# Next chunk's down weights issued behind the fifth product's operands, a gap in phase one's buffers, and the early out projection's split rows kept as two tiles

## The chip, the cores and the metric

The kernel runs on one core of a Trainium2 chip. The metric is the time of one execution on the device, in microseconds (us). Five engines work side by side, each in its own program order: TensorE (PE, matmuls; PEld is its weight loading), VectorE (DVE), ScalarE (ACT), GpSimd (POOL) and SyncE (SP), which here only issues DMA transfers. They wait for each other through semaphores.

## The reference, cut to what matters

A decoder of two layers on 1024 tokens of width 1024, in float32. Each layer is

```python
h = rms_norm(x, attn_norm[l])
proj = h @ w_in[l]
q_a, k_a, v_a, u_b, cq_c, ckv_c, kr_c = jnp.split(proj, split_idx, axis=-1)
out_a = swa_mixer(q_a, k_a, v_a, ...)     # sliding window of 128, 6 heads
out_b = pool_mixer(u_b, ...)              # trailing means over 2, 4, 8, 16
out_c = mla_mixer(cq_c, ckv_c, kr_c, ...) # causal latent attention, 6 heads
mixed = jnp.concatenate([out_a, out_b, out_c], axis=-1)   # width 1024
x = x + mixed @ w_out[l]
h = rms_norm(x, ffn_norm[l])
x = x + (jax.nn.silu(h @ w_gate[l]) * (h @ w_up[l])) @ w_down[l]   # hidden width 2816
```

## The kernel before, in words

Every float32 operand of a matmul is split into two parts, hi (a rounding cast on ScalarE) and lo (operand minus hi, a subtract on VectorE); the helper `split` (L58) does both. A product is then three matmuls: hi·hi, hi·lo and lo·hi.

A layer runs through four stages. Phase one makes the norm, the input projection with weights `wb` and `wa` and the first two mixers. Phase two makes the latent attention; the out projection is done in two parts there: `early_out` (rows 0 to 4 of the eight k-tiles, the first two mixers' output, L890) and `late_out` (the rest). `early_out` is issued at a low priority (offset -3000), so that its matmuls come in between those of the attention. For each of 2 column halves and 8 token tiles it splits five k-tiles of `xm` into one tile `mh` of 128 x 2 x 5 x 128, takes 15 matmuls (L886 to L888, in `outmm`) into `po`, adds `po` to the residual `stage` on VectorE (L907) and stores it. Its `mh` has one buffer in the pool `low`.

Then `gate_up` and `down` make the feed-forward part by a scheme of seven products of half-size blocks in place of eight. `gate_up` writes the token operands of the down products, already split, to a scratch `gd` in device memory (`gd<-go`, L1278).

`down` runs over 11 pairs of row blocks of `w_down` in four chunks of 2, 3, 3 and 3 pairs. A chunk does seven products in the order 1, 2, 5, 6, 3, 7, 4, each of 4 token tiles x its pairs x 3 matmuls, 24 in the first chunk and 36 in the others. What the text calls the fifth product is the fifth in this order (product 3), the sixth is product 7. A product needs

- its token operand `ga`, one 512 KB load per pair (L1041, from `gd`, issued by SyncE),
- its weight operand `op`, a cast on ScalarE (L1043) and a subtract on VectorE (L1044) of a block of `rw`, for some products after subtracts of blocks on GpSimd (L1034).

`rw` are the chunk's weight rows, 512 KB each (L1026): 4 for the first chunk, 6 for each of the others, in two buffers. The first chunk also reads back the residual rows (`xm<-xp`, L1050), and drains `kept`, the last pair's splits and stores of `gate_up` (the `go` subtracts on VectorE, `gd<-go` on SyncE).

The order on each engine is made by a scheduler from the order in which the program is written, its priorities and a simulated time. Of the loads, all are issued by SyncE in that order. A DMA may be tied behind another instruction by `tc.issue_after(...)`. Buffers lie in pools that are placed one behind the other; `gap` (L51) opens a pool that holds nothing but a filler of a given number of bytes per partition, written once by a one-element memset on GpSimd. Phase one has two, of 1024 and 2176 bytes.

Of the kernel before, what the change touches and what calls it, by code (L numbers as in the profile page):

```python
# [12 lines left out]
F32R = mybir.dt.float32r  # L13
# [8 lines left out]
P = 128  # L22
# [303 lines left out]
def phase1(nc, tc, A, l, pool, split, f, bcast, G):  # L326
    ve, sc, gp, te, sy = nc.vector, nc.scalar, nc.gpsimd, nc.tensor, nc.sync
    cosT, sinT = G["cosT"], G["sinT"]
    ident, xm, xrow, krr = G["ident"], G["xm"], G["xrow"], G["krr"]
    with ExitStack() as ph:  # L330
        gap = G["gap"]
# [14 lines left out]
        hp = [pool(ph, f"p1h_{l}"), hq]  # L346
        early = pool(ph, f"p1e_{l}")
        wj = pool(ph, f"p1j_{l}")
        wt = pool(ph, f"p1t_{l}")
        wz = pool(ph, f"p1z_{l}")  # L350
        ps_mm = pool(ph, f"p1mm_{l}", bufs=2, space=PSUM)
# [21 lines left out]
        hTs, rows = {}, {}  # L373
        behind = []
        ahead = {}
# [20 lines left out]
        with tc.high_priority() if l == 0 else nullcontext():  # L396
# [4 lines left out]
            for i, (c0, n) in enumerate(((0, 512), (512, 400), (912, 400))):  # L401
                for k in range(KT):
                    raw = early.tile([P, 512], F32, name="raw", bufs=5 if l else 11)[:, 0:n]
                    dma(raw, A["w_in"][l, k * P : (k + 1) * P, c0 : c0 + n])
                    hi, lo = wcol(0, k, c0, n), wcol(1, k, c0, n)
# [30 lines left out]
        for t in range(NT):  # L436
# [3 lines left out]
            hT, r = hTs[t], rows[t]  # L440
# [41 lines left out]
            for a in range(2):  # L482
                top, low = slice(64 * a, 64 * a + 64), slice(64 - 64 * a, 128 - 64 * a)
# [60 lines left out]
            if t % 2 == 1:  # L544
                W = 16 + 2 * P
                for k in range(2):
# [26 lines left out]
                    po = ps_o.tile([P, 512], F32, name="po")  # L573
# [16 lines left out]
            for g in range(2):  # L590
# [3 lines left out]
                for i0, ni in ((0, 2), (2, 1)):  # L594
                    s = ps_sc.tile([P, 2, 256], F32, name="s")
                    for i in range(i0, i0 + ni):
                        h = 3 * g + i
# [6 lines left out]
                for i in range(3):  # L604
                    h = 3 * g + i
# [3 lines left out]
                for i in range(3):  # L609
                    h = 3 * g + i  # L610
# [19 lines left out]
def phase2(nc, tc, A, l, pool, split, f, bcast, G):  # L630
# [3 lines left out]
    with ExitStack() as ph:  # L634
# [248 lines left out]
        def outmm(po, mh, ml, wo, nk):  # L883
            for k in range(nk):
                wh, wl = wo[k]
                te.matmul(po, mh[:, k], wh, start=k == 0, stop=False)  # L886
                te.matmul(po, mh[:, k], wl, start=False, stop=False)  # L887
                te.matmul(po, ml[:, k], wh, start=False, stop=k == nk - 1)  # L888

        def early_out():  # L890
            for n in range(2):
                c = slice(512 * n, 512 * n + 512)
                wo = []
                for k in range(5):
                    raw = stage(512)
                    rows(raw, k, c)
                    w = (fill if k else low).tile([P, 2, 512], F32R, name=f"wo{k}")
                    split(w[:, 0], w[:, 1], raw)
                    wo.append((w[:, 0], w[:, 1]))
                for t in range(NT):  # L900
                    xt = stage(512)
                    sy.dma_start(xt, G["xsrc"][t * P : (t + 1) * P, c])
                    mh = low.tile([P, 2, 5, P], F32R, name="mh")
                    split(mh[:, 0], mh[:, 1], xm[:, t, 0:5])
                    po = ps_p.tile([P, 512], F32, name="po3")
                    outmm(po, mh[:, 0], mh[:, 1], wo, 5)
                    ve.tensor_tensor(out=xt, in0=xt, in1=po, op=ALU.add)  # L907
                    sy.dma_start(xp[t][:, c], xt)

# [91 lines left out]
def down(nc, tc, A, l, pool, split, f, G, banks, gd, xres, out):  # L1001

    ve, sc, gp, te, sy = nc.vector, nc.scalar, nc.gpsimd, nc.tensor, nc.sync
    xrow, xp = G["xrow"], G["xp"][l]
    last = l == DEPTH - 1
    LEFT, RIGHT = slice(0, 512), slice(512, 1024)
    with ExitStack() as ph:  # L1010
        sg = pool(ph, f"p5s_{l}", bufs=4)
        ac = pool(ph, f"p5a_{l}")
        a1 = ac.tile([P, 4, 512], F32, name="a1")
        a5 = ac.tile([P, 4, 512], F32, name="a5")
        a6 = ac.tile([P, 4, 512], F32, name="a6")
        even = pool(ph, f"p5e_{l}", bufs=2)
        G["go"] = pool(ph, f"p5g_{l}", bufs=2)
        sw = pool(ph, f"p5w_{l}", bufs=3, side="right")

        def load(ps, rp):  # L1020
            h = len(ps)
            rw = rp.tile([P, 2 * h, D], F32, name="rw")
            for b in range(2):
                for j, i in enumerate(ps):
                    r = (2 * i + b) * P
                    sy.dma_start(rw[:, b * h + j], A["w_down"][l, r : r + P, :])  # L1026
            q = {f"B{a + 1}{b + 1}": rw[:, a * h : a * h + h, c] for a in range(2) for b, c in enumerate((LEFT, RIGHT))}
            return ps, q, h

        def chunk(loaded, first, final, ahead=None):  # L1030
            ps, q, h = loaded

            def sub(o, a, b):
                gp.tensor_tensor(out=o, in0=a, in1=b, op=ALU.subtract)  # L1034

            ops, nxt = {}, []

            def operands(at, p, b):
                ga = sg.tile([P, 3, 2, 512], F32R, name="ga")
                for j, i in enumerate(ps):  # L1040
                    sy.dma_start(f(ga[:, j]), gd[i][at])  # L1041
                t = sw.tile([P, 2, 3, 512], F32R, name="op")[:, :, 0:h]
                sc.copy(t[:, 0], q[b])  # L1043
                ve.tensor_tensor(out=t[:, 1], in0=q[b], in1=f(t[:, 0]), op=ALU.subtract)  # L1044
                ops[p] = ga, t

            def rows(ts, n):
                if first:
                    for t in ts:
                        sy.dma_start(xrow[t], xp[t])  # L1050
                    for _ in range(n):
                        next(G["kept"], None)

            operands(0, 1, "B11")
            operands(1, 2, "B21")
            rows(range(4), 0)
            sub(q["B12"], q["B12"], q["B11"])
            operands(2, 5, "B12")
            rows(range(4, 6), 7)
            if ahead is not None:  # L1060
                nxt.append(ahead())
            sub(q["B12"], q["B22"], q["B12"])
            operands(3, 6, "B12")
            rows(range(6, 8), 0)
            if first:
                for t in range(4, NT):
                    gp.tensor_tensor(out=xrow[t][:, LEFT], in0=xrow[t][:, LEFT], in1=xrow[t][:, RIGHT], op=ALU.subtract)
            sub(q["B11"], q["B12"], q["B11"])
            sub(q["B21"], q["B21"], q["B12"])
            operands(4, 3, "B22")  # L1070
            operands(5, 7, "B11")
            operands(6, 4, "B21")

            def add(o, a, eng=ve):
                eng.tensor_tensor(out=o, in0=o, in1=a, op=ALU.add)

            for at, p in enumerate((1, 2, 5, 6, 3, 7, 4)):
                S_, T_ = ops[p]
                for i in range(4):
                    lo, hi = xrow[i], xrow[i + 4]  # L1080
                    n = 4 * at + i
                    acc = banks[n % 8 > 4].tile([P, 512], F32, name="dn", tag=("gu", "dn")[n % 8 > 4])
                    ts = slice(i * P, (i + 1) * P)
                    for j in range(h):
                        te.matmul(acc, S_[:, j, 0, ts], T_[:, 0, j], start=j == 0, stop=False)  # L1085
                        te.matmul(acc, S_[:, j, 0, ts], T_[:, 1, j], start=False, stop=False)  # L1086
                        te.matmul(acc, S_[:, j, 1, ts], T_[:, 0, j], start=False, stop=j == h - 1)  # L1087
                    dst = (a1[:, i], lo[:, LEFT], lo[:, RIGHT], hi[:, LEFT], a5[:, i], a6[:, i], hi[:, RIGHT])[p - 1]
                    if first and p in (1, 5, 6):
                        sc.copy(dst, acc)  # L1090
                    else:
                        add(dst, acc)
                    if not final:
                        continue
                    if p == 1:
                        add(lo[:, LEFT], a1[:, i], gp)
                    elif p == 6:
                        add(a6[:, i], a1[:, i], gp)
                        add(hi[:, LEFT], a6[:, i], gp)
                        add(a5[:, i], a6[:, i], ve)  # L1100
                        add(lo[:, RIGHT], a5[:, i], ve)
                    elif p == 7:
                        add(hi[:, LEFT], hi[:, RIGHT], ve)
                        add(hi[:, RIGHT], a5[:, i], ve)
                    if p in (3, 4):
                        t = i if p == 3 else i + 4
                        dst = out[0] if last else xres
                        sy.dma_start(dst[t * P : (t + 1) * P, :], xrow[t])
            return nxt

        with ExitStack() as st:
            first = load(range(0, 2), pool(st, f"p5z_{l}", side="right"))
            nxt = chunk(first, True, False, lambda: load(range(2, 5), even))
        nxt = chunk(nxt[0], False, False, lambda: load(range(5, 8), even))
        nxt = chunk(nxt[0], False, False, lambda: load(range(8, 11), even))
        chunk(nxt[0], False, True)


# [271 lines left out]
```

## Time and profile before

| what | value |
|---|---|
| median of 3 runs | 2178.31 us (2177.22 to 2181.81) |
| profiled execution, its own time | 2177.97 us |
| its span in the trace | 2176.1 us |
| mean granted clock of TensorE | 0.99 |
| matmul stretch of `down`, layer 0 | 874.4 to 1090.5 us |
| matmul stretch of `down`, layer 1 | 1956.0 to 2171.2 us |
| stretch of `early_out`'s blocks, layer 0 and 1 | about 170 to 345, 1259 to 1425 us |

The page names an instruction by its line, engine, and what it writes and reads (`dn<-op,ga`: the down product's sum from weight operand and token operand). Times in a timeline are microseconds from the span's start. The number in brackets behind a row is the time for which the engine stood idle before it, with the instruction or transfer that ended the wait. DMA rows on SyncE show the issue; "us to landing" is from issue until the data is there.

### The profile page before, as it was taken

Reading aid. Unit: us, or ns where it says so; the run is one execution under the profiler, and the core shown is the slowest. Engines: PE = TensorE matmul, PEld = TensorE weight load, DVE = VectorE, ACT = ScalarE, POOL = GpSimd, SP = SyncE. Lnnn points to the kernel's source line nnn. Section 1 sums busy time; section 2 is a strip of 40 time slices with the busy share of each in tenths; the row PEclk is TensorE's granted clock in tenths of the full one; section 3 lists DMA queues with packets and bytes.
Section 4 is the critical chain, followed back from the end, with each engine's and each line's share of the span. In section 5 each row is a group of like instructions: output and inputs, shape, how many; then the busy total and the mean of one; then the engine's idle time right before and its main releaser. Section 6 shows DMA issues by size and latency. Waiting matters only on the chain.

```text
span 2176.1 us, 29696 instructions
## 1 busy us (share of the span) xinstructions
PE 2096.3 (96%) x10423; PEld 1756.8 (81%) x10423; DVE 1689.1 (78%) x2595; ACT 1084.4 (50%) x2301; POOL 976.0 (45%) x916
## 2 busy tenths in 40 slices
PE   8998999999999999999989989999999999999999
PEld 6886898877888888788878868888778888887887
DVE  6567888799888887765756678887998878877657
ACT  7777676663434333321267777766534443333111
POOL 2445456256544452522624354552654545436215
PEclk9999999999999999999999999999999999999999
DMA  7002211324445335975530122113144344369754
GB/s 232 1 1 97 92 45 49 117 87 145 164 144 176 136 136 194 411 300 196 204 105 1 37 93 83 49 59 128 69 158 169 138 156 151 140 229 406 272 200 164
DMA packets 133732, 312.16 MB, mean 143 GB/s; under 512 B 13071, under 2 KB 63952, under 8 KB 133584
## 3 DMA queue, kind: packets, MB, share of 16 engines
q1 hardware_dynamic: 133396, 310.19, 39.8%
q8 instruction: 83, 1.36, 0.2%
q14 instruction: 65, 0.53, 0.1%
q10 hardware_dynamic: 188, 0.08, 0.0%
HBM read 203.53 MB, written 106.70 MB: 143 GB/s over the span
## 4 chain that ended last, share of the span: by engine, by line
PE 45%; DVE 7%; DMA 5%; issue 2%; ACT 2%; POOL 1%; SPq 0%; DVEq 0%; ACTq 0%; POOLq 0%
PE dn L1085 5%; PE dn L1086 5%; PE dn L1087 5%; PE gu L1240 5%; PE gu L1239 5%; PE gu L1238 5%; PE acc L446 2%; PE acc L447 2%; PE acc L448 2%; DMA ga<-gd 1%; DMA rw<-in_w_down_dram 1%; PE tp L847 1%; PE po L888 1%; PE po L886 1%; PE po L887 1%
## 5 line engine op out<-in xcount | busy, mean ns | idle before, releaser
L1240 PE MATMUL gu<-T,sb 128*128 128x512 f32 x704 | 274.8, 391 | 9.0 <-DVE sb L58 8.8
L1238 PE MATMUL gu<-T,sb 128*128 128x512 f32 x704 | 274.9, 390 | 4.9 <-DVE B L58 2.0
L1239 PE MATMUL gu<-T,sb 128*128 128x512 f32 x704 | 274.0, 389 | 0.0
L1085 PE MATMUL dn<-op,ga 128*128 128x512 f32 x616 | 240.6, 392 | 8.5 <-DMA ga<-gd 8.5
L1086 PE MATMUL dn<-op,ga 128*128 128x512 f32 x616 | 240.7, 391 | 0.0
L1087 PE MATMUL dn<-op,ga 128*128 128x512 f32 x616 | 239.9, 391 | 0.0
L58 ACT CAST go<-xm 128x512 fp32r<-128x512 f32 x154 | 94.8, 620 | 264.5 <-POOL xm L1272 98.6
L1034 POOL TENSOR_TENSOR rw<-rw 128x1536 f32<-128x1536 f32 (+1 forms) x32 | 110.9, 3477 | 245.3 <-DVE op L1044 156.3
L1043 ACT CAST op<-rw 128x1536 fp32r<-128x1536 f32 (+1 forms) x56 | 76.9, 1376 | 284.9 <-PE dn L1087 266.6
L1215 POOL TENSOR_TENSOR xm<-raw 128x512 f32<-128x512 f32 x44 | 68.1, 1550 | 322.3 <-DMA raw<-in_w_up_dram 110.5
L58 DVE TENSOR_TENSOR go<-xm,go 128x512 fp32r<-128x512 f32 x154 | 155.8, 1021 | 34.2 <-ACT go L58 30.1
L58 ACT CAST sb<-raw 128x512 fp32r<-128x512 f32 x180 | 110.1, 617 | 118.0 <-PE gu L1240 97.2
L1240 PEld LDWEIGHTS gu<-T,sb 128*128 128x128 f32 x704 | 132.1, 188 | 40.4 <-DVE sb L58 13.1
L1238 PEld LDWEIGHTS gu<-T,sb 128*128 128x128 f32 x704 | 132.1, 188 | 35.2 <-ACT sb L58 3.5
L58 DVE TENSOR_TENSOR sb<-raw,sb 128x512 fp32r<-128x512 f32 x180 | 157.2, 874 | 1.3 <-ACT sb L58 0.3
L1272 POOL TENSOR_TENSOR xm<-xm 128x512 f32<-128x512 f32 x88 | 142.6, 1628 | 30.1 <-DVE go L58 19.3
L1239 PEld LDWEIGHTS gu<-T,sb 128*128 128x128 f32 x704 | 132.2, 188 | 27.2
L1044 DVE TENSOR_TENSOR op<-rw,op 128x1536 fp32r<-128x1536 f32 (+1 forms) x56 | 114.4, 2044 | 39.1 <-ACT op L1043 36.1
L1085 PEld LDWEIGHTS dn<-op,ga 128*128 128x128 f32 x616 | 116.4, 189 | 34.5 <-issue 7.3
L1087 PEld LDWEIGHTS dn<-op,ga 128*128 128x128 f32 x616 | 116.2, 189 | 24.6
L1086 PEld LDWEIGHTS dn<-op,ga 128*128 128x128 f32 x616 | 116.5, 189 | 24.0
L1238 PE MATMUL gu<-B,A 128*128 128x512 f32 x336 | 131.5, 391 | 2.8 <-ACT B L58 2.8
(332 smaller groups left out, 6071.4 us busy)
## 6 DMA issues: line engine op xcount, KB each, us to landing
gd<-go SPq DMA_DIRECT2D x154, 512.0 KB, 3.1
ga<-gd SPq DMA_DIRECT2D x154, 512.0 KB, 5.9
raw<-in_w_gate_dram SPq DMA_DIRECT2D x22, 1024.0 KB, 5.6
raw<-in_w_up_dram SPq DMA_DIRECT2D x22, 1024.0 KB, 6.2
rw<-in_w_down_dram SPq DMA_DIRECT2D x44, 512.0 KB, 8.7
xp<-stage SPq DMA_DIRECT2D x32, 256.0 KB, 2.0
old<-xp SPq DMA_DIRECT2D x16, 512.0 KB, 4.2
xp<-xm SPq DMA_DIRECT2D x16, 512.0 KB, 2.9
```

What stands on the lines that cost most here:

```text
L58: return sc.copy(hi, src), ve.tensor_tensor(out=lo, in0=src, in1=f(hi), op=ALU.subtract)
L1034: gp.tensor_tensor(out=o, in0=a, in1=b, op=ALU.subtract)
L1043: sc.copy(t[:, 0], q[b])
L1044: ve.tensor_tensor(out=t[:, 1], in0=q[b], in1=f(t[:, 0]), op=ALU.subtract)
L1085: te.matmul(acc, S_[:, j, 0, ts], T_[:, 0, j], start=j == 0, stop=False)
L1086: te.matmul(acc, S_[:, j, 0, ts], T_[:, 1, j], start=False, stop=False)
L1087: te.matmul(acc, S_[:, j, 1, ts], T_[:, 0, j], start=False, stop=j == h - 1)
L1215: gp.tensor_tensor(out=s1, in0=q["A21"], in1=q["A22"], op=ALU.add)
L1238: te.matmul(acc, s[:, 0, k], b[:, 0, k], start=k == 0, stop=False)
L1239: te.matmul(acc, s[:, 0, k], b[:, 1, k], start=False, stop=False)
L1240: te.matmul(acc, s[:, 1, k], b[:, 0, k], start=False, stop=k == HK - 1)
L1272: gp.tensor_tensor(out=q[o], in0=q[a], in1=q[b], op=op)
```

## The change

It has three parts. In `down`, the loading of the next chunk's weights moves from behind the third product's operands to behind the fifth's, and each of its transfers is tied behind the one before it, the first behind the last `ga` load of the fifth product; the second group of residual rows moves behind the fourth product's operands. In phase one a third filler of 384 bytes is opened ahead of the pools of `wa` and of most of `wb`. In `early_out`, the split rows are kept as two tiles, `mh0` with three k-tiles and `mh3` with two, each with its own cast and subtract, of the same size together as `mh`.

```diff
@@ phase one
         wj = pool(ph, f"p1j_{l}")
+        gap(ph, f"p1m_{l}", 384)
         wt = pool(ph, f"p1t_{l}")
@@ early_out
-                    mh = low.tile([P, 2, 5, P], F32R, name="mh")
-                    split(mh[:, 0], mh[:, 1], xm[:, t, 0:5])
+                    parts = []
+                    for a, b in ((0, 3), (3, 5)):
+                        mh = low.tile([P, 2, b - a, P], F32R, name=f"mh{a}")
+                        split(mh[:, 0], mh[:, 1], xm[:, t, a:b])
+                        parts += [(mh[:, 0, k], mh[:, 1, k]) for k in range(b - a)]
                     po = ps_p.tile([P, 512], F32, name="po3")
-                    outmm(po, mh[:, 0], mh[:, 1], wo, 5)
+                    for k in range(5):
+                        (hi, lo), (wh, wl) = parts[k], wo[k]
+                        te.matmul(po, hi, wh, start=k == 0, stop=False)
+                        te.matmul(po, hi, wl, start=False, stop=False)
+                        te.matmul(po, lo, wh, start=False, stop=k == 4)
@@ down, load
-        def load(ps, rp):
+        def load(ps, rp, pin=None):
...
-                    sy.dma_start(rw[:, b * h + j], A["w_down"][l, r : r + P, :])
+                    with tc.issue_after(pin.ins) if pin else nullcontext():
+                        pin = sy.dma_start(rw[:, b * h + j], A["w_down"][l, r : r + P, :])
@@ down, chunk
+            pin = []
...
-                    sy.dma_start(f(ga[:, j]), gd[i][at])
+                    pin[:] = [sy.dma_start(f(ga[:, j]), gd[i][at])]
...
             operands(2, 5, "B12")
-            rows(range(4, 6), 7)
-            if ahead is not None:
-                nxt.append(ahead())
             sub(q["B12"], q["B22"], q["B12"])
             operands(3, 6, "B12")
+            rows(range(4, 6), 7)
             rows(range(6, 8), 0)
...
             operands(4, 3, "B22")
+            if ahead is not None:
+                nxt.append(ahead(pin[0]))
             operands(5, 7, "B11")
             operands(6, 4, "B21")
```

SyncE in the first chunk of `down` of layer 0, from the second `ga` load of the fourth product on (the names `gd_0_4` and `gd_1_4` are the fifth product's operands of pairs 0 and 1, `gd_10_0` a store by `gate_up`), in the program of before:

```order
L1041 DMA ga<-gd_1_3_5617 128x1024
L1050 DMA xm<-xp_83 128x1024
L1026 DMA rw<-in_w_down_dram 128x1024 x3
L1050 DMA xm<-xp_84 128x1024
L1278 DMA gd_10_0_5677<-go 128x1024
L1050 DMA xm<-xp_85 128x1024
L1026 DMA rw<-in_w_down_dram 128x1024 x2
L1278 DMA gd_10_1_5678<-go 128x1024
L1026 DMA rw<-in_w_down_dram 128x1024 x2
L1041 DMA ga<-gd_0_4_5611 128x1024
L1041 DMA ga<-gd_1_4_5618 128x1024
L1026 DMA rw<-in_w_down_dram 128x1024 x5
```

The same place in the program of the change:

```order
L1051 DMA ga<-gd_1_3_5671 128x1024
L1060 DMA xm<-xp_83 128x1024
L1060 DMA xm<-xp_84 128x1024
L1288 DMA gd_10_0_5731<-go 128x1024
L1060 DMA xm<-xp_85 128x1024
L1288 DMA gd_10_1_5732<-go 128x1024
L1051 DMA ga<-gd_0_4_5665 128x1024
L1051 DMA ga<-gd_1_4_5672 128x1024
L1035 DMA rw<-in_w_down_dram 128x1024 x6
L1051 DMA ga<-gd_0_5_5666 128x1024
L1051 DMA ga<-gd_1_5_5673 128x1024
L1288 DMA gd_10_2_5733<-go 128x1024
```

The seven weight rows ahead of the fifth product's operands are gone from there, and six stand between those and the sixth product's.

VectorE at the same time, from the third product's weight split on (`op`, L1044; `go` is `gate_up`'s last token operand, `xm<-xm,dn` the adding of a product's result), before:

```order
L1044 TENSOR_TENSOR op<-rw,op 128x1024
L1075 TENSOR_TENSOR xm<-xm,dn 128x512 x4
L1044 TENSOR_TENSOR op<-rw,op 128x1024
L58 TENSOR_TENSOR go<-xm,go 128x512
L1044 TENSOR_TENSOR op<-rw,op 128x1024
L58 TENSOR_TENSOR go<-xm,go 128x512
L1044 TENSOR_TENSOR op<-rw,op 128x1024
```

And with the change:

```order
L1054 TENSOR_TENSOR op<-rw,op 128x1024
L1085 TENSOR_TENSOR xm<-xm,dn 128x512 x4
L58 TENSOR_TENSOR go<-xm,go 128x512
L1054 TENSOR_TENSOR op<-rw,op 128x1024
L58 TENSOR_TENSOR go<-xm,go 128x512
L1054 TENSOR_TENSOR op<-rw,op 128x1024 x2
```

A `go` subtract now stands ahead of the next weight split, and the last two splits follow each other.

TensorE in an early block of `early_out` of layer 0 (`po` is the block's sum, `wo` its weights; L621 and L622 belong to the sliding-window mixer), before:

```order
L886 MATMUL po_3269<-wo_3193,mh 128x512
L887 MATMUL po_3269<-wo_3193,mh 128x512
L621 MATMUL po<-pT,vt 128x384
L888 MATMUL po_3269<-wo_3193,mh 128x512
L886 MATMUL po_3269<-wo_3199,mh 128x512
L887 MATMUL po_3269<-wo_3199,mh 128x512
```

And with the change:

```order
L912 MATMUL po_3284<-wo_3211,mh_3278 128x512
L913 MATMUL po_3284<-wo_3211,mh_3278 128x512
L914 MATMUL po_3284<-wo_3211,mh_3278 128x512
L622 MATMUL po<-pT,vt 128x384
L912 MATMUL po_3284<-wo_3216,mh_3281 128x512
L913 MATMUL po_3284<-wo_3216,mh_3281 128x512
```

All 15 matmuls of a block read one `mh` before; now the first nine read one tile and the last six another, and a matmul of the mixer stands between the two.

More of the change, by code (lines that the diff above doesn't have):

```diff
@@ L1112, in down @@
             first = load(range(0, 2), pool(st, f"p5z_{l}", side="right"))
-            nxt = chunk(first, True, False, lambda: load(range(2, 5), even))
-        nxt = chunk(nxt[0], False, False, lambda: load(range(5, 8), even))
-        nxt = chunk(nxt[0], False, False, lambda: load(range(8, 11), even))
+            nxt = chunk(first, True, False, lambda pin: load(range(2, 5), even, pin))
+        nxt = chunk(nxt[0], False, False, lambda pin: load(range(5, 8), even, pin))
+        nxt = chunk(nxt[0], False, False, lambda pin: load(range(8, 11), even, pin))
         chunk(nxt[0], False, True)
```

## The prediction

> **What bounds the kernel now.** I read the page of before first: busy times, then the costliest groups of TensorE and their idle, then TensorE's list of waits, which splits that idle by releaser.
>
> ```profile
> PE 2096.3 (96%) x10423; PEld 1756.8 (81%) x10423; DVE 1689.1 (78%) x2595; ACT 1084.4 (50%) x2301; POOL 976.0 (45%) x916
> PE dn L1085 <- DMA ga<-gd: 8.5, 4, 3.3
> PE po L888 <- DVE mh L58: 2.0, 2, 1.3
> PE po L886 <- DVE stage L907: 2.0, 1, 2.0
> ```
>
> TensorE is busy for 96% of a span of 2176.1 us (1.9 us less than the execution's own 2177.97), so the end moves when one of its gaps closes or opens, or when its clock changes. The change adds and removes no matmul. It touches three of these waits: 8.5 us in four waits for token operands `ga` of the down products, and 2.0 us for each of the early out projection's `mh` and `stage`.
>
> The timeline of TensorE shows the four waits, two in each layer (start, duration, then the idle time before it and its releaser in brackets).
>
> ```profile
> 896.11 0.39 PE L1087 MATMUL dn<-op,ga 128*128 128x512 f32 x1
> 897.99 0.47 PE L1085 MATMUL dn<-op,ga 128*128 128x512 f32 x1 [1.49 <-DMA ga<-gd]
> ...
> 903.29 0.39 PE L1087 MATMUL dn<-op,ga 128*128 128x512 f32 x1
> 906.95 0.76 PE L1085 MATMUL dn<-op,ga 128*128 128x512 f32 x1 [3.27 <-DMA ga<-gd]
> ...
> 1977.58 0.39 PE L1087 MATMUL dn<-op,ga 128*128 128x512 f32 x1
> 1978.45 0.47 PE L1085 MATMUL dn<-op,ga 128*128 128x512 f32 x1 [0.48 <-DMA ga<-gd]
> ...
> 1983.79 0.39 PE L1087 MATMUL dn<-op,ga 128*128 128x512 f32 x1
> 1987.41 0.47 PE L1085 MATMUL dn<-op,ga 128*128 128x512 f32 x1 [3.23 <-DMA ga<-gd]
> ```
>
> The restarts at 897.99 and 1978.45 are the fifth product's first matmuls, those at 906.95 and 1987.41 the sixth's. What follows each long wait is in the windows (length, then busy us of PE, PEld, DVE, ACT and POOL with instructions, granted clock, DMA share, GB/s).
>
> ```profile
> 906.95:909.64 2.69, 2.69 (x6) 2.12 (x7) 0.03 (x1) 0.00 (x0) 0.00 (x0) 0.50 1.02 408
> 1988.64:1991.60 2.96, 2.96 (x9) 2.28 (x8) 0.00 (x0) 0.00 (x0) 0.00 (x0) 0.51 1.04 419
> 876.80:932.00 55.20, 50.44 (x215) 40.77 (x214) 40.34 (x34) 18.99 (x26) 34.68 (x14) 0.97 1.02 407
> 929.00:1060.00 131.00, 131.00 (x580) 108.47 (x579) 79.25 (x87) 25.75 (x18) 42.63 (x15) 1.00 0.63 230
> ```
>
> An undisturbed matmul is one step of 131 / 580 = 0.226 us (last row). Start to start, less that step, the four waits lose 1.65 and 3.43 us in layer 0, 0.64 and 3.39 us in layer 1. After each gap of 3.2 us the granted clock is half for almost 3 us: six matmuls start in 2.69 us in place of 6 x 0.226, a loss of 1.33; in layer 1 seven start in 2.96 us (two of the nine in the row began earlier), a loss of 1.38. **What the waits cost: 1.65 + 3.43 + 1.33 = 6.41 us in layer 0, 0.64 + 3.39 + 1.38 = 5.41 us in layer 1, 11.8 us together.**
>
> Why `ga` is late: from 876.8 to 932 the sixteen DMA engines are fully busy at 407 GB/s, so one 512 KB transfer costs 524 KB / 407 GB/s = 1.28 us. SyncE's timeline and one piece of the chain of waits show the order in which they were issued.
>
> ```profile
> 877.25 1.31 SPq L1026 DMA_DIRECT2D rw<-in_w_down_dram  x3
> ...
> 884.36 0.99 SPq L1026 DMA_DIRECT2D rw<-in_w_down_dram  x2
> 886.81 0.33 SPq L1278 DMA_DIRECT2D gd<-go  x1
> 887.18 1.28 SPq L1026 DMA_DIRECT2D rw<-in_w_down_dram  x2
> 888.56 0.89 SPq L1041 DMA_DIRECT2D ga<-gd  x2
> 890.26 5.38 SPq L1026 DMA_DIRECT2D rw<-in_w_down_dram  x5
> ...
> 896.64 10.18 DMA ga<-gd
> ```
>
> Seven weight rows `rw` stand ahead of the fifth product's `ga` (888.56), all twelve ahead of the sixth's, whose first is issued at 896.64 and takes 10.18 us, eight turns of 1.28, to land at 906.82, where TensorE restarts. They are six for each of the next two chunks, and the first of those starts only behind the seventh product. So what ends last here is a queue of bytes in the wrong order.
>
> **The change, part by part.** *Down weights.* The same twelve transfers of 512 KB are issued in another place: the next chunk's six behind the fifth product's `ga` of this chunk, the other six behind that of the next. Bytes stay; nothing is added on an engine. Landings in layer 0, by the row of a store alone:
>
> ```profile
> gd<-go SPq DMA_DIRECT2D x154, 512.0 KB, 3.1
> ```
>
> SyncE still can't pass the store of 886.81, which waits for DVE; `ga` follows it. With no `rw` ahead, only five transfers (three `xm` rows and two stores, 6.4 us of work) stand in the ten us before, so the store lands at about 886.8 + 3.1 = 889.9. At 1.28 us apiece in issue order: fifth product's `ga` 891.2 and 892.5 (TensorE can take them one step after 896.11, at 896.3); six `rw` to 900.1; sixth's `ga` 901.4 and 902.7 (needed one product of 24 steps, 5.4 us, later: 901.8; the second pair's, 12 matmuls later, 904.5); two stores; seventh's `ga` 906.5 and 907.8 (needed from 907.2); the next chunk's first three by 911.7 (needed from 912.7). The margins are 5.1, 0.4, 0.7 and 1.0 us. In layer 1 both waits of before were shorter (0.64 and 3.39), so I take its margins as no smaller. So all 11.8 us should go, with 0 to 2 us of them back where a margin of half a us fails; I take 0.4. The half-clock windows go with the long gaps. The six late `rw`, and those of the later chunks, are in stretches of 63% DMA share (929 to 1060), where a transfer has room.
>
> Next late behind the removed wait is VectorE's split of the fourth operand. The changed order lets a `go` subtract pass it.
>
> ```profile
> 888.95 2.47 DVE L1075 TENSOR_TENSOR xm<-xm,dn 128x512 f32<-128x512 f32 x4
> 891.34 3.39 DVE L1044 TENSOR_TENSOR op<-rw,op 128x1024 fp32r<-128x1024 f32 x1
> 894.65 1.77 DVE L58 TENSOR_TENSOR go<-xm,go 128x512 fp32r<-128x512 f32 x1
> ```
>
> The fifth product's split, due at 896.3, would start at 891.4 + 1.8 = 893.2 and end between 895.5 (2.3 us, what the same form took when it was short) and 896.5: 0 to 0.2 us of stall. That is in the 0.4.
>
> *Gap.* One POOL memset per layer and 384 bytes of addresses.
>
> ```profile
> 1074.38 0.10 POOL L52 MEMSET gap<- 128x1 f32 x1
> L448 PE MATMUL acc<-wb,hT x48: 290/346/398, 1202.2 to 1258.2; 128*128 128x512 f32 x24, 128*128 128x288 f32 x24
> L773 ACT ACTIVATE vT<-acc,rc x2: 574/578/581, 1296.9 to 1297.8; 128x384 fp32r<-128x384 f32 x2
> ```
>
> The same kind of memset costs 0.10 us, beside a POOL at 45%. The shift puts another `wb` tile under phase two's `vT`; `wb` is last read at 1258.2, `vT` first written at 1296.9, so 38 us of cover stand behind a cost of nothing. If that went, each us by which `vT` waits costs one.
>
> *Two tiles for the split rows.* Each of 32 blocks of the early out projection gets a cast and a subtract of 3 k-tiles and one of 2, in place of one of 5: 32 more casts, 32 more subtracts. No new wait is for data; but the last six matmuls now wait for the second subtract, and the first nine only for the first.
>
> ```profile
> L58 DVE TENSOR_TENSOR mh<-xm,mh 128x640 fp32r<-128x640 f32 x16 | 13.1, 820 | 5.2 <-ACT mh L58 4.9
> L58 DVE TENSOR_TENSOR cl<-xm,ch 128x384 fp32r<-128x384 f32 x14 | 7.7, 549 | 0.0
> L601 DVE TENSOR_TENSOR Pt<-s,bias 128x256 f32<-128x256 f32 x6 | 2.5, 413 | 0.0
> L58 ACT CAST mh<-xm 128x640 fp32r<-128x640 f32 x15 | 10.9, 727 | 14.9 <-PE po L888 14.8
> L58 ACT CAST ch<-xm 128x384 fp32r<-128x384 f32 x14 | 7.1, 512 | 1.1 <-PE tp L887 0.5 <-PE acc L738 0.3 <-PE ss L738 0.2
> L58 ACT CAST ch<-xm 128x256 fp32r<-128x256 f32 x2 | 0.8, 406 | 1.6 <-PE tp L887 1.4 <-DVE xm L861 0.2
> ```
>
> More work: DVE 549 + 413 - 820 = 142 ns a block, 2.3 us a layer; ACT 512 + 406 - 727 = 191 ns, 3.1 us a layer. The windows of the two stretches say how much cover there is.
>
> ```profile
> 170.00:345.00 175.00, 160.91 (x957) 139.91 (x955) 145.12 (x341) 128.29 (x333) 97.20 (x122) 0.97 0.21 72
> 1259.00:1425.00 166.00, 154.00 (x914) 133.76 (x912) 138.79 (x326) 122.31 (x321) 94.32 (x121) 0.97 0.19 66
> 217.53 0.80 PE L888 MATMUL po<-wo,mh 128*128 128x512 f32 x1 [1.26 <-DVE mh L58]
> ```
>
> DVE has 30 and 27 us free, ACT 47 and 44: the extra work fits beside TensorE. Bounds of the whole edit: as a gain, the waits for `mh` and `stage` of before, 2.0 + 2.0 us, and at the far end all of TensorE's idle, 14.1 and 12.0 us; as a loss, the added work in full, 2 x (2.3 + 3.1) = 10.8 us. I take nothing, nearest to the rows that show the added work small against free time.
>
> [...]
>
> Sum: 2177.97 - 11.8 + 0.4 + 0 = **2166.6 us**. The execution shown lies 0.3 us below the median, 2178.31, so the forecast for the median is as good as the same.
>
> **The rivals.**
>
> *Partial relief (2168 to 2173).* Six `rw` still stand ahead of the sixth `ga`, with 0.4 us of margin. If all in flight share the engines, each transfer behind the burst ends later than my list: the second `ga` of the sixth, requested when the one eight ahead lands (892.5, or some 3 us later if that one shares too) and 10.2 us in flight, lands between 902.7 and 906 against 904.5. A stall of 1.5 us in each layer gives 2166.6 + 3.0 = 2169.6; if that of layer 0 grows to the old length with its half clock, 3.43 + 1.33 + 1.5 = 6.3 give 2172.9. Against: the 10.18 us of before are eight turns of 1.28, as a queue served in order gives them. [...]
>
> *The attention stretches pay (2174 to 2179).* The scheduler's order of TensorE, DVE and ACT changes from the first early block on; if the added casts and subtracts come in full on the path, 2166.6 + 10.8 = 2177.4. For: ACT and DVE are at 73 to 84% there. Against: TensorE idles 26 us there already and the extra is spread over 340 us.
>
> *Slower (2183 to 2190).* TensorE works in order. In a block whose second split queues on DVE behind attention's work, the tenth matmul blocks all attention matmuls behind it. The place is each block's first matmul from the second tile; the price is the 1.26 us of the row at 217.53; it decides from 13 of the 32 blocks, 16.4 us, and at 16 gives 2166.6 + 20.2 = 2186.8. For: the split is two hops, ACT then DVE. Against: only two of 32 blocks waited so before.
>
> *The early projection fills better (2153 to 2162).* The first nine matmuls can start after a smaller cast and subtract, and a second buffer is free sooner: the 4.0 us of `mh` and `stage` waits go, and some of the 26 us idle: 2162.6 down to 2166.6 - 13 = 2153.6.
>
> *The weights don't move in time.* If the chip issues as before, 2178; SyncE's order is fixed in the program, so I give it nothing of its own.
>
> **How the numbers follow.** Forecast (2162 to 2170) 0.56; partial relief 0.11; the stretches pay 0.12; slower 0.07; fills better 0.14. The range of 8 in 10 reaches up through partial relief and half of the paying stretches, 2176, and down to 2157 into the better filling. About 4.4 us, 0.2%, is what a measurement of this kernel can tell from no change: faster means below 2173.9, slower above 2182.7. Forecast, partial relief and better filling are faster, 0.81; the paying stretches are mostly within, 0.12; slower 0.07.
>
> **What would show it.** TensorE's list has no wait for `ga` over 0.5 us, no half-clock window at 907 and 1989, and each down stretch is some 6 and 5 us shorter; SyncE's timeline has the fifth's `ga` straight behind the second store. DVE gains 4.5 us and ACT 6.2. A TensorE idle of 14 and 12 us in the two attention stretches, within 4, shows the split as free; over 20 shows it wrong. The prediction is wrong if `ga` of the sixth is late by over 2 us, or if those stretches lengthen.

## The result, and the profile after

| | median, us | runs | lowest to highest |
|---|---|---|---|
| before | 2179.56 | 4 | 2177.22 to 2181.81 |
| changed | 2165.09 | 4 | 2164.02 to 2169.80 |

The ratio is 0.994, with a 95% interval of 0.9926 to 0.9954: 10 to 16 us faster. The forecast was 2166.6 us in a range of 2157 to 2176. The profiled execution of the changed kernel took 2169.8 us (span 2168.0), the slowest of its four, which matters below.

The busy times of the changed kernel's page, and from its list of what TensorE waited for (total, times, longest, in us) the lines on the three waits that the prediction spoke of, with the one between the layers:

```profile
PE 2101.5 (97%) x10423; PEld 1763.3 (81%) x10423; DVE 1699.9 (78%) x2627; ACT 1088.1 (50%) x2333; POOL 978.1 (45%) x918
PE th L391 <- DVE xm L1085: 3.2, 1, 3.2
...
PE po L914 <- DVE mh L58: 0.6, 1, 0.6
...
PE dn L1095 <- DMA ga<-gd: 0.3, 1, 0.3
...
PE po L912 <- DVE stage L915: 0.2, 1, 0.2
```

The wait for `ga` is down from 8.5 us in four to 0.3 us in one, those for `mh` and `stage` together from 4.0 to 0.8. SyncE's timeline in layer 0 shows why the first is gone:

```profile
886.17 0.32 SPq L1288 DMA_DIRECT2D gd<-go  x1
886.58 2.20 SPq L1051 DMA_DIRECT2D ga<-gd  x2
888.83 2.91 SPq L1035 DMA_DIRECT2D rw<-in_w_down_dram  x6
891.84 1.35 SPq L1051 DMA_DIRECT2D ga<-gd  x2
894.24 1.60 SPq L1288 DMA_DIRECT2D gd<-go  x2
896.81 5.40 SPq L1051 DMA_DIRECT2D ga<-gd  x5
```

The fifth product's operands stand straight behind the store that waits for VectorE, and only six weight rows stand ahead of the sixth's (issued from 891.84). What is left of the waits, in TensorE's timeline, is at the sixth product:

```profile
901.33 0.39 PE L1097 MATMUL dn<-op,ga 128*128 128x512 f32 x1
902.01 0.47 PE L1095 MATMUL dn<-op,ga 128*128 128x512 f32 x1 [0.30 <-DMA ga<-gd]
```

The table shows where the time went in all profiles of this study. A stage lasts from the start of its first matmul (in layer 0's phase one, the first of the input projection) to that of the next stage's first, `down` to that of its own last, so that the stretches add up to the span (13 us at its two ends are left out). "Gaps" is TensorE's idle time ahead of matmuls over the whole span. "Half clock" is an estimate from the start times: for each matmul of 256 columns or more with no gap behind it, a step of 1.6 to 2.4 times a warm one counts with what it is longer than a warm one.

| profile | phases 1+2, layer 0 | gate_up 0 | down 0 | to layer 1, phases 1+2 | gate_up 1 | down 1 | gaps | half clock | span |
|---|---|---|---|---|---|---|---|---|---|
| before | 433.9 | 432.1 | 216.2 | 434.0 | 431.6 | 215.1 | 70.1 | 26.0 | 2176.1 |
| changed | 432.7 | 433.3 | 210.0 | 437.9 | 431.6 | 209.2 | 56.9 | 31.8 | 2168.0 |
| e1 down only | 433.5 | 433.2 | 210.0 | 437.4 | 432.7 | 209.2 | 62.5 | 26.6 | 2169.3 |
| e2 split only | 427.4 | 432.2 | 215.5 | 436.4 | 434.6 | 216.9 | 66.8 | 29.9 | 2176.0 |
| e3 gap only | 433.9 | 433.4 | 217.3 | 433.8 | 431.9 | 215.2 | 72.4 | 27.9 | 2178.6 |
| e4 changed | 427.0 | 433.1 | 209.8 | 433.9 | 433.4 | 209.2 | 58.6 | 26.1 | 2159.3 |
| e5 behind fourth | 429.3 | 434.5 | 209.3 | 433.7 | 432.8 | 209.2 | 59.6 | 24.6 | 2161.9 |
| e6 behind sixth | 427.7 | 433.4 | 212.8 | 437.8 | 433.8 | 211.2 | 65.9 | 24.6 | 2169.9 |
| e7 one tile | 432.7 | 434.2 | 209.6 | 440.3 | 432.5 | 209.8 | 66.1 | 26.9 | 2172.2 |
| e8 layer 0 split | 431.7 | 432.8 | 209.7 | 442.9 | 433.1 | 209.2 | 66.6 | 23.5 | 2172.6 |
| e9 behind fourth | 429.4 | 433.0 | 209.3 | 434.4 | 432.9 | 209.2 | 58.1 | 25.3 | 2161.2 |
| e10 changed | 431.7 | 434.4 | 210.3 | 438.0 | 433.3 | 209.2 | 61.3 | 29.8 | 2169.8 |

Of the first pair, the two down stretches shrink by 6.1 and 5.9 us. The span shrinks by only 8.1, since the stretch up to layer 1's `gate_up` is 3.9 us longer. Over the whole span the gaps fall by 13.2 us and the half clock grows by 5.8.

### The profile page after: what moved, and what is told of

The parts are those of the page before. It is cut to its first block, busy times and chain, and to the rows that moved or that the text cites. A ratio compares the mean times of both kernels' runs of the same rounds, so it can differ in the third digit from the quotient of the medians.

```text
span 2168.0 us, 29758 instructions
## 1 busy us (share of the span) xinstructions
PE 2101.5 (97%) x10423; PEld 1763.3 (81%) x10423; DVE 1699.9 (78%) x2627; ACT 1088.1 (50%) x2333; POOL 978.1 (45%) x918
## 4 chain that ended last, share of the span: by engine, by line
PE 75%; DVE 10%; DMA 5%; ACT 5%; POOL 3%; issue 2%; SPq 0%; POOLq 0%; DVEq 0%; ACTq 0%
PE gu L1250 10%; PE gu L1248 10%; PE gu L1249 10%; PE dn L1095 6%; PE dn L1097 6%; PE dn L1096 6%; PE acc L447 3%; PE acc L448 3%; PE acc L449 3%; PE tp L848 2%; PE po L912 1%; PE po L914 1%; PE po L913 1%; PE ss L824 1%; DVE sb L58 1%
## 5 line engine op out<-in xcount | busy, mean ns | idle before, releaser
L1054 DVE TENSOR_TENSOR op<-rw,op 128x1536 fp32r<-128x1536 f32 (+1 forms) x56 | 119.0, 2124 | 41.8 <-ACT op L1053 41.8
```

## The experiments

### The three parts alone, and the change again

Each part alone, on one chip with 23 runs of before (median 2181.01 us). e1 takes the hunks of `down`, e2 those of `early_out`, e3 this one line; e4 is the changed kernel as it is.

```diff
         wj = pool(ph, f"p1j_{l}")
+        gap(ph, f"p1m_{l}", 384)
```

> Only the edits of the down stage: the next chunk's weights behind the fifth product's token operands, the residual rows behind the fourth's. Theory (the four waits for ga and their half-clock windows were all of it): the two down stretches of TensorE shrink by about 6 us each, to 210.0 and 209.2 us as in the changed kernel, nothing else moves, 12 us faster than before (ratio 0.9945). Rival (part of the gain comes from the other two edits, or the down stage gives some back elsewhere): under 9 us faster.

> Only the early out projection's split rows as two tiles. Theory of the prediction (the added casts and subtracts lie beside TensorE): within 2 us of before, idle of TensorE in the two attention stretches as before within 4 us. Rival 1 (early projection fills better): 3 to 8 us faster. Rival 2 (the added work or new half-clock windows cost): 3 to 10 us slower.

> Only the filler of 384 bytes in phase one; every engine's order is as before but for one memset per layer on POOL. Theory (0.1 us of POOL, address overlaps with 38 us of cover): within 1 us of before. Rival (a wait of layer 1's phase one on the down stage's buffers ends earlier, since its weights lie elsewhere): 1 to 3 us faster, all of it between 1090 and 1260 us.

> The changed kernel once more, for a second profile. In the first profiled execution (2169.8 us, the slowest of four) TensorE ran at half clock at 508.8 and from 1434.7 to 1443.3 us, which cost 4.8 us and which the profile of before doesn't have. Theory (such windows differ from execution to execution): about 2165 us, and without at least one of the two. Rival (they belong to the changed order): both are there again and the time is near 2169.

| | median, us | runs | ratio | interval | less before's median |
|---|---|---|---|---|---|
| e1 down only | 2170.77 | 6 | 0.9951 | 0.9938 to 0.9965 | -10.2 |
| e2 split only | 2178.62 | 12 | 0.9989 | 0.9978 to 1.0 | -2.4 |
| e3 gap only | 2180.18 | 12 | 0.9994 | 0.9985 to 1.0004 | -0.8 |
| e4 the change | 2166.79 | 6 | 0.9933 | 0.9918 to 0.9948 | -14.2 |

The parts add up: 10.2 + 2.4 + 0.8 = 13.4 of 14.2 us.

e1: the theory held. The down stretches are 209.97 and 209.21 us, 12.1 us together less than before's, and the time falls by 10.2, with 7.6 to 13.5 in the interval. Something is given back behind it: the stretch from there to layer 1's `gate_up` is 3.4 us longer in e1's profile than in before's (437.4 against 434.0). Of these, 0.6 us are in plain sight: the wait of layer 1's first transposes for the last sums of layer 0 is 3.2 us in place of 2.6, since they start behind the last of VectorE's two closing sums, no longer behind the one ahead of it. All later profiles but e3's have the same 3.2. The other 2.8 us aren't explained; e4, with the same edits of `down`, has a stretch of 433.9.

e2: the result lies between the theory (within 2 us) and the first rival (3 us or more). The median is 2.4 us lower, with 0 to 4.8 in the interval. It is shown that the edit isn't slower; its gain is at the edge of what 12 runs tell. Its one profile can't settle it: the gaps are 3.3 us smaller than before's, the half clock is 3.9 us longer, and the span is the same.

e3: nothing that 12 runs could tell (3.3 us faster to 0.9 slower). The rival's place shows nothing either: the stretch up to layer 1's `gate_up` is 433.8 us against before's 434.0.

Two points follow from the programs themselves, in which the order on each engine is fixed. With the residual rows put back to where they were, the order on every engine is that of the change: their move is inert. With the loading moved but not tied (`ahead(None)`), the order is that of a program without the down edits: the scheduler takes the loads to the front again. **It is the tie behind the `ga` load that moves the weights; a move of the call alone leaves the order as it was.**

e4 gives the same program in 2161.1 us where the first profile took 2169.8. From the windows (busy us of PE, PEld, DVE, ACT and POOL, granted clock, DMA share, GB/s) of the first and of e4:

```profile
1434.70:1443.30 8.60, 8.60 (x30) 7.40 (x29) 3.79 (x6) 3.11 (x6) 4.92 (x4) 0.50 0.01 2
508.80:511.80 3.00, 3.00 (x9) 2.31 (x8) 3.00 (x5) 1.58 (x3) 1.28 (x1) 0.50 1.04 356
```

```profile
1425.40:1431.40 6.00, 6.00 (x23) 5.32 (x22) 2.31 (x3) 1.85 (x4) 4.48 (x3) 0.50 0.01 3
...
502.00:506.00 4.00, 4.00 (x19) 3.31 (x18) 4.00 (x6) 1.77 (x3) 1.55 (x2) 1.00 0.89 282
```

The long half-clock stretch of layer 1's attention is 6.0 us in e4 in place of 8.6, and that of `gate_up` isn't there: 502 to 506 is the same place, at full clock. The theory held for one of the two, and the time was nearer to its figure than to the rival's.

### Where the weights stand in the queue

e5 ties the next chunk's rows behind the fourth product's operands, e6 behind the sixth's (`operands(5, 7, "B11")`); the rest is the change. The edit of e5:

```diff
             operands(3, 6, "B12")
+            if ahead is not None:
+                nxt.append(ahead(pin[0]))
...
             operands(4, 3, "B22")
-            if ahead is not None:
-                nxt.append(ahead(pin[0]))
```

> The change with the next chunk's six weight rows tied behind the fourth product's token operands instead of the fifth's. On SyncE they now stand ahead of the fifth's ga again, six in place of before's seven, and six in place of twelve ahead of the sixth's. Theory A (bytes ahead in the queue count): ga of the fifth lands one transfer of 1.28 us earlier than before, at about 896.6, a wait of 0 to 0.5 us in layer 0; the sixth's lands six transfers earlier, at about 899, no wait; no half-clock window, stretches 209.5 to 210.5 us, as fast as the change within 1 us. Rival B (any weight row ahead of the fifth's operands makes it late): waits for the fifth of 1.5 us or more in layer 0 come back, 2 to 4 us slower than the change.

> The change with the weight rows tied behind the sixth product's token operands. The change still has one short wait for ga, 0.30 us at 902.01, and two late steps behind it. Theory: that wait goes, the first stretch of down is 209.3 to 209.8 us (210.0 and 209.75 in the two profiles of the change); the next chunk's splits have rows 3 us later and still end in time. Rival: the rows, landing until about 905, make the next chunk's first weight operand late, a wait of 0.5 us or more near 912.7.

| | median, us | runs | ratio | interval |
|---|---|---|---|---|
| e5 behind the fourth's | 2163.42 | 4 | 0.9926 | 0.9913 to 0.9938 |
| e6 behind the sixth's | 2172.01 | 4 | 0.9963 | 0.9948 to 0.9978 |

e5, SyncE in layer 0:

```profile
873.75 0.32 SPq L1060 DMA_DIRECT2D xm<-xp  x1
874.18 3.12 SPq L1035 DMA_DIRECT2D rw<-in_w_down_dram  x6
878.29 2.93 SPq L1060 DMA_DIRECT2D xm<-xp  x2
881.32 2.71 SPq L1288 DMA_DIRECT2D gd<-go  x2
884.12 5.95 SPq L1051 DMA_DIRECT2D ga<-gd  x6
```

Theory A held in the trace: no wait for `ga` is left, and the first down stretch is 209.25 us, 0.8 less than in the change's first profile. Rival B fell: six weight rows stand ahead of the fifth's operands without harm. They go out at 874 to 877, while SyncE would stand and wait for the stores of `go`, and all the operands follow. So the cause was narrower than "weight rows ahead of the fifth", as far as one run tells that changes the rows' number and their moment at once: with the tie, the second next chunk's six rows no longer come along, and the first six use the time in which nothing else could be issued.

e6: both theory and rival missed; the first down stretch is 212.8 us. TensorE waits at two places in layer 0; SyncE's timeline and VectorE's stand behind:

```profile
901.71 0.39 PE L1097 MATMUL dn<-op,ga 128*128 128x512 f32 x1
903.45 0.47 PE L1095 MATMUL dn<-op,ga 128*128 128x512 f32 x1 [1.35 <-DMA ga<-gd]
...
923.74 0.39 PE L1097 MATMUL dn<-op,ga 128*128 128x512 f32 x1
925.79 0.50 PE L1095 MATMUL dn<-op,ga 128*128 128x512 f32 x1 [1.67 <-DVE xm L1085]
```

```profile
881.36 2.81 SPq L1051 DMA_DIRECT2D ga<-gd  x4
884.22 0.66 SPq L1035 DMA_DIRECT2D rw<-in_w_down_dram  x1
886.17 0.32 SPq L1288 DMA_DIRECT2D gd<-go  x1
886.53 3.02 SPq L1035 DMA_DIRECT2D rw<-in_w_down_dram  x5
891.63 0.33 SPq L1288 DMA_DIRECT2D gd<-go  x1
893.25 4.06 SPq L1051 DMA_DIRECT2D ga<-gd  x4
```

```profile
920.30 4.84 DVE L1054 TENSOR_TENSOR op<-rw,op 128x1536 fp32r<-128x1536 f32 x1 [0.89 <-ACT op L1053]
925.07 1.27 DVE L1085 TENSOR_TENSOR xm<-xm,dn 128x512 f32<-128x512 f32 x2
```

The sixth's operands are in time, but now the seventh's stand behind six rows and a store (893.25) and are 1.35 us late. The second wait, in both layers, is for VectorE's sum, which frees the buffer that the next matmul writes: VectorE's order has a weight split of 4.84 us ahead of it. As for the first wait, the displaced transfers find the next reader.

### What the two tiles are worth

```diff
-                    parts = []
-                    for a, b in ((0, 3), (3, 5)):
-                        mh = low.tile([P, 2, b - a, P], F32R, name=f"mh{a}")
-                        split(mh[:, 0], mh[:, 1], xm[:, t, a:b])
-                        parts += [(mh[:, 0, k], mh[:, 1, k]) for k in range(b - a)]
+                    mh = low.tile([P, 2, 5, P], F32R, name="mh")
+                    for k in (slice(0, 3), slice(3, 5)):
+                        split(mh[:, 0, k], mh[:, 1, k], xm[:, t, k])
+                    parts = [(mh[:, 0, k], mh[:, 1, k]) for k in range(5)]
```

> The change, but the two casts and two subtracts of the early out projection write two parts of one tile mh, as large as before's; the added instructions stay, the second buffer goes. Theory (the 1 to 2 us a layer that the split edit saves in TensorE's gaps come from the tiles' separate release and separate readiness): the gaps of the two attention stretches go back towards 18 us each, 1 to 3 us slower than the change. Rival (they come from the smaller pieces or from another order alone): gaps of 16 to 17 us as with two tiles, no slower than the change.

2173.96 us (7 runs), ratio 0.9961, interval 0.9947 to 0.9976. What the theory forecast came, by more than its size: e7 is 6.3 us faster than before, where the change was 14.5, 14.2 (e4) and 10.9 (e10) faster, and the gaps of the whole span are 66.1 us where the change's three profiles have 56.9 to 61.3. In e7's list of waits the two of before are back:

```profile
PE po L911 <- DVE stage L914: 1.9, 1, 1.9
...
PE po L913 <- DVE mh L58: 1.8, 1, 1.8
```

So smaller pieces alone don't help: by the medians e7 is even behind e1, which has neither split nor gap and was 10.2 us faster than before (the two intervals overlap). TensorE's gaps in phases one and two of both layers together say the same: 46.1 to 48.1 us in the three profiles with one tile (before, e1, e3), 42.0 to 45.3 in the seven with two tiles in both layers, 49.7 in e7. The half clock in these stretches is no shorter with two tiles, about 21 to 29 us against 22 to 24. That the gain comes from each tile's becoming ready and free on its own is the likeliest reading, but not shown apart from another: from about 190 us on, TensorE, VectorE and ScalarE have another order in e7 than in the change, since the scheduler made a new one around the single tile.

### Layer 0 alone, and the better place once more

e8 is e5 with `for a, b in ((0, 5),) if l else ((0, 3), (3, 5))`; e9 is e5 again, e10 the change again.

> Weights behind the fourth product, gap, and the two tiles in layer 0 only; layer 1's blocks keep one tile of five. In the profiles so far the two-tile order is 4.9 us shorter than the one-tile order in layer 0's phases one and two together (428.8 against 433.8 us, means of five and three profiles), but 0.5 us longer in layer 1's (431.0 against 430.4): its gaps are 2.9 us smaller, its half-clock steps 3.2 us longer. Theory (the split edit earns its time in layer 0 alone): as fast as with both layers split within 2 us. Rival (layer 1's smaller gaps count, its half clock was chance): 2 to 4 us slower than the same kernel with both layers split, which runs beside it.

> Weights behind the fourth product, gap and both layers split, once more, beside the run above and for another profile: 2161 to 2167 us; no wait for ga, down stretches 209.2 to 209.8 us.

> The change a third time, on the same chip as the two above: 0 to 2 us slower than with the weights behind the fourth product (0.75 us of its first down stretch, the rest chance).

| | median, us | runs | ratio | interval |
|---|---|---|---|---|
| e8 layer 0 split only | 2173.37 | 7 | 0.9962 | 0.9948 to 0.9975 |
| e9 behind the fourth's | 2163.22 | 5 | 0.9923 | 0.991 to 0.9936 |
| e10 the change | 2170.23 | 5 | 0.9949 | 0.9937 to 0.9961 |

e8's theory fell. In the profiles, layer 1 with one tile is 442.9 us up to `gate_up`, against 433.7 and 434.4 in e5 and e9, and e8 is 10.2 us slower than e9, more than even the rival had. But before, with one tile in both layers, had 434.0 there. The orders of the engines in layer 1 differ among all three, so what one tile costs in layer 1 depends on the order that the scheduler makes around it; which instruction of that order costs the 9 us stays open.

e9's expectation held: 2163.22 us, no wait for `ga`, down stretches of 209.33 and 209.21 us; it repeats e5 within 0.2 us. e10's missed: the change beside it was 7.0 us slower in place of 0 to 2, and the intervals of the ratio don't overlap. The two profiles are 8.6 us apart. About 1 us of that is in the first down stretch (210.27 against 209.33). 5.9 us lie in phases one and two and 1.8 in `gate_up`, where both programs have the same order on every engine. The half clock is 29.8 us over the span against 25.3, so it is the larger part. Why it is shorter in both profiles of the faster program isn't settled, and chance isn't ruled out: over three sets of runs the change has medians of 2165.1 to 2170.2, and its fastest profile (e4, span 2159.3) is shorter than either of this version's. **This version has the lowest medians of the study, 2163.4 and 2163.2 us, about 17 to 18 us ahead of before; of its lead over the change only the 1 us in `down` has a cause that the traces show.**

## Why the prediction was right

**The waits for `ga`: right in mechanism and size.** The term was 11.8 us; the down stretches of the four profiles with the change's down part (the changed kernel, e1, e4 and e10) are 11.8 to 12.3 us shorter together, and no half-clock window is left in them. Of the landings, the sixth's first was put at 901.4 against a need of 901.8; TensorE was ready at 901.56 and restarted at 902.01, a slip of half a us, which the 0.4 in the sum stood for. One need in the list is wrong: a pair's second operand is put 12 matmuls behind its first, but the loop goes over the pairs inside each token tile, so it is needed three matmuls, 0.7 us, behind. By the list's own landings the sixth's second pair would then have been 0.2 us late (902.7 against 902.5). TensorE starts on it at 902.78, without a wait, so nothing came of it.

**The closeness of the total is in part luck.** The forecast of 2166.6 us starts from an execution of before of 2177.97; before's four runs beside the changed kernel have a median of 2179.56. As a difference, 11.4 us were forecast, and 14.5 measured (10 to 16), then 14.2 in e4 and 10.9 in e10.

**Its reason was a little too wide.** The prediction read the fault as seven and twelve rows ahead of the operands, and took the new place as the cure. e5 shows that six rows ahead of the fifth's operands, issued early, do nothing; and without the tie the order is the old one. What is left as the harm is that the rows of two chunks were let out together in the one saturated stretch (in before, 876.8 to 932: DMA share 1.02, 407 GB/s).

**The gap: right**, nothing measurable.

**The two tiles: taken as nothing, measured as a gain of 2.4 us (0 to 4.8).** The added instructions cost what the rows said, or somewhat more. The subtracts and casts by form in layer 0 of the changed kernel (busy us, mean ns, idle before):

```profile
L58 DVE TENSOR_TENSOR mh<-xm,mh 128x384 fp32r<-128x384 f32 x16 | 9.5, 591 | 5.9 <-ACT mh L58 5.8
L58 DVE TENSOR_TENSOR mh<-xm,mh 128x256 fp32r<-128x256 f32 x16 | 6.8, 426 | 0.5 <-ACT mh L58 0.4
```

591 + 426 - 820 = 197 ns a block, where 142 was forecast. Over both layers the instructions on `mh` take 5.9 us more of VectorE and 6.3 us more of ScalarE, where 4.5 and 6.2 were forecast. But the added work lay beside TensorE, and most of the waits for `mh` and `stage` went, as the rival of the early projection filling better said: 4.0 us before, 0.8 in the changed kernel, up to 2.4 in its other profiles. In the likeliest case their going was left out of the sum; that is the term that was mis-sized, by about 2 us.

Of the signs that were named for this part, the idle of TensorE held. The windows of the changed kernel that match those of before:

```profile
172.00:345.00 173.00, 161.67 (x961) 141.38 (x961) 147.33 (x357) 128.31 (x346) 97.31 (x116) 0.97 0.21 69
1252.00:1420.00 168.00, 157.25 (x909) 136.60 (x909) 138.10 (x340) 124.34 (x332) 92.37 (x115) 0.96 0.19 64
```

TensorE is idle for 11.3 and 10.8 us there, after 14.1 and 12.0 before. These windows are wider than the early projection: its matmuls run from 182.8 to 304.2 and 1263.7 to 1390.3 us before, from 182.4 to 305.7 and 1257.9 to 1384.3 after. Whether these stretches lengthen tells little, since the order changed what lies between: 656 matmuls before and 686 after in layer 0, 695 and 671 in layer 1. The two signs on busy time didn't come as said: by the pages VectorE's rose by 10.8 us in place of 4.5 and ScalarE's by 3.7 in place of 6.2, which the instructions on `mh` don't account for.

**What was missing from the sum is the half clock outside `down`.** It runs from 26.1 to 31.8 us in three profiles of the same program. In the first profile it hid a good part of the gain. The mean granted clock of the single runs goes roughly with it: e4's six runs reach from 2161.1 us at 0.992 to 2170.8 us at 0.987. So one program spreads by some us; how much of this is left in the medians isn't shown.

## What to carry to other kernels

Where one queue is full, count the bytes ahead of the next operand that is read and move those that are read last; and look whether the scheduler moves them back unless they are tied. Before taking away a wait for a tile, ask whether the tile can be ready, and be free again, in two parts. And profile one program more than once before a few us of its trace are explained.

## What the runs showed that was not expected

TensorE's half clock doesn't follow its gaps alone. `gate_up` has in each layer one wait of about 2.06 us with the same work behind it. In before it was followed by full clock:

```profile
508.36 0.50 PE L1240 MATMUL gu<-T,sb 128*128 128x512 f32 x1 [2.07 <-DVE sb L58]
...
508.40:516.00 7.60, 7.60 (x34) 6.29 (x35) 6.88 (x9) 2.78 (x5) 3.87 (x4) 1.00 0.83 293
```

and in the changed kernel, 1.6 us later, by the half clock shown above at 508.80:

```profile
507.18 0.50 PE L1250 MATMUL gu<-T,sb 128*128 128x512 f32 x1 [2.06 <-DVE sb L58]
```

Over the first nine profiles, of eighteen such waits eight were followed by seven to nine slow steps, a loss of 1.2 to 1.7 us each, and ten were not, whatever the kernel. No slow step followed the wait of 1.49 us in `down` of before: the granted clock is 1.00 from 897.99 to 903.52. What decides whether a wait of about 2.06 us is followed by slow steps isn't shown.
